# A 64 KB block of zeros written early to the rows that the first result overwrites, in a rotary-embedding kernel on Trainium2

## The chip, the cores and the metric

The kernel runs on one core of one Trainium2 chip. The metric is the device time of one execution in microseconds (us). "Span" is the profiled execution from its first to its last record; a run's time is about 1.8 us more than its span.

## The reference

```python
def reference(x, cos, sin):            # x: (8, 2048, 16, 64) f32; cos, sin: (2048, 32) f32
    x1, x2 = x[..., :32], x[..., 32:]
    cos, sin = cos[None, :, None, :], sin[None, :, None, :]
    return concatenate([x1 * cos - x2 * sin, x1 * sin + x2 * cos], axis=-1)
```

x has 67.1 MB, and so has the output. Each of the 8 batches is 8.39 MB in float32; the kernel keeps one batch in SBUF as float16, 4096 KB (128 partitions x 32 KB).

## The kernel before

The head of batch 0, sin and cos are loaded in float32 on the SyncE queue. Everything else is moved on the GpSimd queue, which converts float32 to float16 on the way in and back on the way out. ScalarE converts the head, sin and cos; VectorE does four passes per batch.

```python
    NBUF = 5
    ...
    head = const_pool.tile([P, JA, H, D], f32)
    x0 = x[0].rearrange("(p j) h d -> p j (h d)", j=J)
    nc.sync.dma_start(out=head..., in_=x0[:, 0:JA, :]...)              # 1 MB
    sin_f = const_pool.tile([P, J, Dh], f32)
    cos_f = const_pool.tile([P, J, Dh], f32)
    ...
    nc.sync.dma_start(out=sin_f, in_=sin.rearrange("(p j) d -> p j d", j=J))   # 256 KB
    nc.sync.dma_start(out=cos_f, in_=cos.rearrange("(p j) d -> p j d", j=J))   # 256 KB

    def load(b):  ...   # nc.gpsimd.dma_start: x[b] -> xt (f16), 4096 KB; batch 0 without its head
    def store(b, xt):
        nc.gpsimd.dma_start(out=out[b].rearrange("(p j) h d -> p (j h d)", j=J), in_=xt)
    def rotate(xt):     # four VectorE passes; the third is the cosine multiply
        ...
        nc.vector.tensor_mul(out=xw, in0=xw, in1=cos_b)
        nc.vector.tensor_add(out=xa, in0=xa, in1=v...)

    tiles = [load(b) for b in range(NBUF)]
    nc.scalar.copy(out=tiles[0][:, 0:JA, :, :]..., in_=head...)
    nc.scalar.copy(out=sin_h, in_=sin_f)
    nc.scalar.mul(out=neg_h, in_=sin_f, mul=-1.0)
    nc.scalar.copy(out=cos_h, in_=cos_f)
    for b in range(B):
        rotate(tiles[b])
        store(b, tiles[b])
        if b + NBUF < B:
            tiles.append(load(b + NBUF))
```

In the compiled order the GpSimd queue holds five loads, then store 0, store 1, load 5, load 6, store 2, store 3, load 7, stores 4 to 7. Load 5 waits for store 0 to land (its buffer comes free then), load 6 for store 1, load 7 for store 2.

## Time and profile before

| | before |
|---|---|
| median time (6 runs) | 318.21 us (317.96 to 318.41) |
| span of the profiled run | 316.1 us |
| VectorE busy | 209.2 us, 66% |
| DMA engines, both queues | 98.5% + 1.4% of 16 engines' span |
| read + written | 67.63 + 67.11 MB, 426 GB/s |

From the page of the kernel before: the span; busy time of the engines; the slices (one digit is the busy tenths of one fortieth of the span, here 7.9 us); then the DMA queues with packets, MB, and the share of 16 engines' span that their packets took.

```profile
span 316.1 us, 121 instructions
...
DVE 209.2 (66%) x32; ACT 4.9 (2%) x5; POOL 8.8 (3%) x20
...
DVE  0009799999999999999879999990009993000000
...
DMA  9899999999999999999999999999999999999996
...
q0 software_dynamic: 2304, 100.14, 98.5%
q1 hardware_dynamic: 432, 1.57, 1.4%
HBM read 67.63 MB, written 67.11 MB: 426 GB/s over the span
```

The DMA engines are full in all slices but the last, while VectorE (DVE) is idle in the first three and the last six, and in some between. The kernel is bound by the transfers. It follows that a wait on any other engine costs time only if the DMA queues run empty because of it.

DMA issues of the kernel before (output <- input, queue, count, KB each, median us from issue to landing):

```profile
head<-in_x_dram SPq DMA_DIRECT2D x1, 1024.0 KB, 4.8
sin_f<-in_sin_dram SPq DMA_DIRECT2D x1, 256.0 KB, 13.4
cos_f<-in_cos_dram SPq DMA_DIRECT2D x1, 256.0 KB, 31.8
out_dram<-xt POOLq DMA_DIRECT2D x8, 66.0
```

256 KB of cos need 31.8 us, over six times as long as 1 MB of head. The packet records in the trace tell why. There are eight data packets per engine in each of these transfers. (A record names the queue of a packet and not its engine. "Per engine" is here a sixteenth of all packets of a kind; the first or last 16 load or store packets by start are taken for one of each engine.) Head and most of sin pass before the engines take up the loads, between 5.2 and 5.7 us. After that, one packet of cos (2 KB, 96 ns) passes for each load packet (28 KB landed in SBUF, 2.13 us, later 32 KB and 2.43 us). The Trainium skill, "DMA: Bandwidth & Descriptors", section "Queues, rings and completion order", describes this: an engine goes round-robin between its queues, a packet at a time. Here the trace agrees.

Timeline of the kernel before (start, duration, engine, line, operation, and in brackets how long the engine was idle before and what ended it). L58 is a store, L51 a load, L70 the cosine multiply:

```profile
33.51 0.62 ACT L81 CAST cos_h<-cos_f 128x512 f16<-128x512 f32 x1 [17.74 <-DMA cos_f<-in_cos_dram]
34.16 8.69 DVE L70 TENSOR_TENSOR xt<-xt,cos_h 128x16384 f16<-128x16384 f16 x1 [1.75 <-ACT cos_h L81]
...
52.14 0.54 POOL L58 DMA_DIRECT2D out_dram<-xt  x1 [48.10 <-DVE xt L72]
...
78.12 0.54 POOL L58 DMA_DIRECT2D out_dram<-xt  x1 [25.44 <-DVE xt L72]
...
121.76 0.53 POOL L51 DMA_DIRECT2D xt<-in_x_dram  x1 [43.11 <-DMA out_dram<-xt]
...
263.88 0.53 POOL L58 DMA_DIRECT2D out_dram<-xt  x1 [50.50 <-DVE xt L72]
```

Store 0 is issued at 52.1 us, when VectorE is done with batch 0. But the packet records show the store's first packet only at 101.07 us: its descriptors stand in the same queue behind five loads. This distance of 49 us, less the time from an issue to its first packet, is the slack of store 0.

Who waited for whom (us in total, times, longest), first lines of the waits of the kernel before:

```profile
POOL out_dram L58 <- DVE xt L72: 136.3, 4, 50.5
POOL xt L51 <- DMA out_dram<-xt: 118.3, 3, 56.4
...
DVE xt L70 <- ACT cos_h L81: 1.7, 1, 1.7
```

### The profile page before, as it was taken

How to read it: one execution, taken by the hardware profiler on the slowest of the kernel's cores; microseconds unless marked ns; L12 is line 12 of the kernel's file. 1: busy time of each engine (PE TensorE's matmuls, PEld its weight loads, DVE VectorE, ACT ScalarE, POOL GpSimd, SP SyncE). 2: the span in 40 equal slices, each digit the busy share in tenths (PEclk: the TensorE clock that was granted, in tenths of full speed). 3: DMA queues.
4: the chain of work that ended last, by engine and by line, in shares of the span. 5: the costliest groups of instructions: out<-in, count | busy, mean ns of one | idle time of the engine just before them, and what ended most of it. 6: DMA issues, size and time to landing. Idle time of an engine off the chain costs nothing.

```text
span 316.1 us, 121 instructions
## 1 busy us (share of the span) xinstructions
DVE 209.2 (66%) x32; ACT 4.9 (2%) x5; POOL 8.8 (3%) x20
## 2 busy tenths in 40 slices
DVE  0009799999999999999879999990009993000000
ACT  4100000000000000000000000000000000000000
POOL 3000000000000000010000000100000000000000
DMA  9899999999999999999999999999999999999996
GB/s 277 182 261 208 199 236 228 199 199 265 199 199 265 398 506 423 398 336 261 199 199 224 373 398 398 506 423 265 203 328 398 398 448 481 398 398 506 423 398 265
DMA packets 2736, 101.71 MB, mean 322 GB/s; under 512 B 304, under 2 KB 304, under 8 KB 560
## 3 DMA queue, kind: packets, MB, share of 16 engines
q0 software_dynamic: 2304, 100.14, 98.5%
q1 hardware_dynamic: 432, 1.57, 1.4%
HBM read 67.63 MB, written 67.11 MB: 426 GB/s over the span
## 4 chain that ended last, share of the span: by engine, by line
issue 44%; DVE 14%; another core or an unknown queue 14%; DMA 10%; POOL 1%; SPq 0%; ACT 0%; POOLq 0%
DMA cos_f<-in_cos_dram 10%; DVE xt L70 6%; DVE xt L72 6%; DVE v L67 1%; DVE v L68 1%; POOL out_dram L58 1%; POOL xt L51 0%; ACT cos_h L81 0%; POOLq L112 0%; SPq L45 0%; SPq L36 0%; POOLq L58 0%
## 5 line engine op out<-in xcount | busy, mean ns | idle before, releaser
L70 DVE TENSOR_TENSOR xt<-xt,cos_h 128x16384 f16<-128x16384 f16 x8 | 69.5, 8692 | 2.0 <-ACT cos_h L81 1.7
L67 DVE TENSOR_TENSOR v<-xt,neg_h 128x8192 f16<-128x8192 f16 x8 | 35.4, 4426 | 52.2 <-DMA xt<-in_x_dram 52.0
L72 DVE TENSOR_TENSOR xt<-xt,v 128x16384 f16<-128x16384 f16 x8 | 69.5, 8692 | 0.3
L68 DVE TENSOR_TENSOR v<-xt,sin_h 128x8192 f16<-128x8192 f16 x8 | 35.4, 4419 | 0.0
L58 POOL DMA_DIRECT2D out_dram<-xt x8 | 4.3, 535 | 136.3 <-DVE xt L72 136.3
L51 POOL DMA_DIRECT2D xt<-in_x_dram x8 | 4.4, 559 | 119.1 <-DMA out_dram<-xt 118.3
L75 ACT CAST xt<-head 128x2048 f16<-128x2048 f32 x1 | 1.9, 1897 | 3.5 <-DMA head<-in_x_dram 3.5
L75 ACT ACT_TABLE_LOAD x1 | 1.3, 1283 | 0.7 <-PEq L101 0.7
L81 ACT CAST cos_h<-cos_f 128x512 f16<-128x512 f32 x1 | 0.6, 617 | 17.7 <-DMA cos_f<-in_cos_dram 17.7
L79 ACT CAST sin_h<-sin_f 128x512 f16<-128x512 f32 x1 | 0.6, 618 | 7.2 <-DMA sin_f<-in_sin_dram 7.2
L80 ACT ACTIVATE neg_h<-sin_f 128x512 f16<-128x512 f32 x1 | 0.6, 624 | 0.0
L101 POOL MEMSET const-float32-0.0<- 128x1 f32 x1 | 0.1, 98 | 0.2 <-issue 0.2
L101 POOL MEMSET const-bfloat16-1.0<- 128x1 bf16 x1 | 0.1, 101 | 0.0
L101 POOL MEMSET const-float32-1.0<- 128x1 f32 x1 | 0.1, 98 | 0.0
L101 POOL MEMSET const-uint8-127<- 128x1 uint8 x1 | 0.1, 98 | 0.0
## 6 DMA issues: line engine op xcount, KB each, us to landing
xt<-in_x_dram POOLq DMA_DIRECT2D x7, 4096.0 KB, 41.2
xt<-in_x_dram POOLq DMA_DIRECT2D x1, 3584.0 KB, 22.3
head<-in_x_dram SPq DMA_DIRECT2D x1, 1024.0 KB, 4.8
sin_f<-in_sin_dram SPq DMA_DIRECT2D x1, 256.0 KB, 13.4
cos_f<-in_cos_dram SPq DMA_DIRECT2D x1, 256.0 KB, 31.8
out_dram<-xt POOLq DMA_DIRECT2D x8, 66.0
```

The costliest lines, as they stand in the source:

```text
L51: nc.gpsimd.dma_start(out=xt[:, j0:J, :, :].rearrange("p j h d -> p (j h d)"), in_=x[b].rearrange("(p j) h d -> p j (h d)", j=J)[:, j0:J, ...
L58: nc.gpsimd.dma_start(out=out[b].rearrange("(p j) h d -> p (j h d)", j=J), in_=xt)
L67: nc.vector.tensor_mul(out=v[:, :, :, 0:Dh], in0=xt[:, :, :, Dh:D], in1=neg_b)
L68: nc.vector.tensor_mul(out=v[:, :, :, Dh:D], in0=xt[:, :, :, 0:Dh], in1=sin_b)
L70: nc.vector.tensor_mul(out=xw, in0=xw, in1=cos_b)
L72: nc.vector.tensor_add(out=xa, in0=xa, in1=v.rearrange("p j h d -> p (j h d)"))
L75: nc.scalar.copy(out=tiles[0][:, 0:JA, :, :].rearrange("p j h d -> p (j h d)"), in_=head.rearrange("p j h d -> p (j h d)"),)
L79: nc.scalar.copy(out=sin_h, in_=sin_f)
L80: nc.scalar.mul(out=neg_h, in_=sin_f, mul=-1.0)
L81: nc.scalar.copy(out=cos_h, in_=cos_f)
L101: nc = _bacc.Bacc("TRN2", target_bir_lowering=False, num_devices=1)
```

## The change

The result stays the same, as the zeros are overwritten. As far as the diff shows, the intent is to touch the output early, at a time when ScalarE's queue has nothing to do. What it costs, or gains, is asked here.

```diff
+    zero = const_pool.tile([P, 128], f32)
+    nc.vector.memset(zero, 0.0)
+    nc.scalar.dma_start(
+        out=out[0].rearrange("(p j) h d -> p (j h d)", j=J)[:, 0:128], in_=zero
+    )
     sin_f = const_pool.tile([P, J, Dh], f32)
```

Each of the 128 partitions writes 512 B. Store 0 writes the same bytes later, so the compiled store 0 gets one wait more, on the zeros' semaphore. The Trainium skill, "DMA: Bandwidth & Descriptors", section "Two DMAs through the same engine are not ordered", says that such a semaphore is the ordering that a kernel's author has; sharing a queue or an engine does not order the two writes. All other instructions keep their order on each engine. The line numbers after the change are higher by five (L70 becomes L75).

## The prediction

> **What bounds the kernel.** The 16 DMA engines. The page gives software queue q0 98.5% and hardware queue q1 1.4% of the engines' span; VectorE is busy 66% (209.2 us). 67.63 MB are read and 67.11 MB written: 426 GB/s over the 316.1 us span. The packet records add up to about 315.7 us per engine, so the span is the sum of the packets' times; the "issue" shares in the chain of waits are the GpSimd queue waiting for transfers in flight.
>
> **What the change does.** It adds a 128x128 memset on VectorE, idle until 23.65 us (timeline); a 64 KB transfer on the ScalarE queue, 128 rows of 512 B, eight per engine; and, in the compiled order, one wait: the first store also waits for the zeros to land. Nothing is removed; the order on every engine is otherwise the same.
>
> **Cost on the DMA engines.** In the packet records 8 KB packets of the head took 309 ns, 2 KB packets of sin/cos 84 ns. The line through these puts a 512 B packet at 28 ns (estimate): eight, with a completion packet of 9 to 22 ns, are 0.25 us per engine; perhaps 0.5 us if short writes are dearer. The engines are full from 2 us on, so this adds to the sum: +0.25 to +0.5 us.
>
> **The new wait.** The Trainium skill, "DMA: Bandwidth & Descriptors", section "Queues, rings and completion order", says an engine goes round-robin between its queues, a packet at a time. The trace agrees: after the loads start (first packet 5.2 us), one 2 KB packet passes per load packet of 2.13 us (later 2.43), so cos needs 31.8 us to land. The zeros should start at 2 to 2.5 us beside the head's packets and land by 5 to 7 us; caught behind load packets, by about 22 us. The first store becomes ready only at 51.6 us. So the wait is free. Even a late first store has room: its packets queue behind the first five loads, which fill the engines until 101 us (first store packet 101.1 us).
>
> **A side effect.** The zeros take engine time before the loads start. About 3 to 5 packets of sin/cos per engine then move behind load packets: sin lands at 21 to 25 us instead of 14.6, cos at 40 to 44 instead of 33.5, and the cosine multiply starts at 41 to 45 instead of 34.2. VectorE's early chain slides up to 10 us; the first two stores issue at about 60 and 87 instead of 52.1 and 78.1, both before 101 us. The third and fourth were issued only at 141.6 anyway, and the last (ready 263.6, its packets starting near 295) keeps slack. So this is absorbed: DMA never runs dry.
>
> **Predicted time: 318.5 us, range 318.0 to 319.3** (8 in 10). Faster by over 2%: 0.01; within 2%: 0.965; slower by over 2%: 0.025.
>
> **What would show each step.** A memset under 0.3 us near 1 us; zeros landing before 25 us; no wait of the first store put down to the zeros, but to the last add; cos landing later, the cosine multiply's idle time up from 1.75 us to around 10; DMA share still 98% or more; the sixth load still issued near 121.8 us; the last store landing 0.3 to 0.5 us later.
>
> **What would make it wrong.** Short strided writes costing far more than 28 ns; zeros landing after 52 us, or after 100 us, so that engines run dry before the first store; the slide of VectorE's chain exceeding its slack late; a fixed launch cost of a third DMA-issuing queue.

## The result, and the profile after

| | before | after |
|---|---|---|
| median time, 6 runs each | 318.21 us | 317.95 us |
| lowest to highest | 317.96 to 318.41 | 317.87 to 318.63 |
| ratio, 95% interval | | 0.9997, 0.9984 to 1.001 |
| span of the profiled run | 316.1 us | 316.1 us |

A ratio is the mean time of one kernel's fast runs over that of the other's fast runs of the same rounds, so it is not quite the ratio of the medians. The change is within noise: the interval reaches from 0.5 us less to 0.3 us more. The median is 0.05 us under the lower end of the predicted range.

The same lines of the page of the kernel after; q10 is the ScalarE queue:

```profile
span 316.1 us, 125 instructions
...
DVE 209.3 (66%) x33; ACT 4.9 (2%) x5; POOL 8.9 (3%) x20
...
DVE  0009179999999999999999999993009993000000
...
DMA  9899999999999999999999999999999999999996
...
q0 software_dynamic: 2304, 100.14, 98.4%
q1 hardware_dynamic: 432, 1.57, 1.4%
q10 hardware_dynamic: 144, 0.07, 0.1%
HBM read 67.63 MB, written 67.17 MB: 426 GB/s over the span
```

The DMA row has the same digits. In the DVE row the fifth digit fell from 7 to 1: that is the longer wait for cos. The memset adds 0.1 us to VectorE in this rounding, and the new queue took 0.1% of the engines' span.

DMA issues of the kernel after:

```profile
head<-in_x_dram SPq DMA_DIRECT2D x1, 1024.0 KB, 4.9
sin_f<-in_sin_dram SPq DMA_DIRECT2D x1, 256.0 KB, 19.9
cos_f<-in_cos_dram SPq DMA_DIRECT2D x1, 256.0 KB, 39.2
out_dram<-xt POOLq DMA_DIRECT2D x8, 59.6
out_dram<-zero ACTq DMA_DIRECT2D x1, 64.0 KB, 4.8
```

The zeros landed 4.8 us after their issue at 1.03 us, so at 5.8 us. Sin and cos landed 6.5 and 7.4 us later than before.

Timeline of the kernel after, the lines that answer to those of before and the two new ones:

```profile
0.84 0.17 DVE L41 MEMSET zero<- 128x128 f32 x1 [0.84 <-PEq L106]
1.03 0.40 ACTq L42 DMA_DIRECT2D out_dram<-zero  x1
...
40.86 0.62 ACT L86 CAST cos_h<-cos_f 128x512 f16<-128x512 f32 x1 [18.64 <-DMA cos_f<-in_cos_dram]
41.51 8.69 DVE L75 TENSOR_TENSOR xt<-xt,cos_h 128x16384 f16<-128x16384 f16 x1 [8.77 <-ACT cos_h L86]
...
59.49 0.54 POOL L63 DMA_DIRECT2D out_dram<-xt  x1 [55.44 <-DVE xt L77]
...
85.47 0.54 POOL L63 DMA_DIRECT2D out_dram<-xt  x1 [25.44 <-DVE xt L77]
...
121.76 0.54 POOL L56 DMA_DIRECT2D xt<-in_x_dram  x1 [35.76 <-DMA out_dram<-xt]
...
263.92 0.53 POOL L63 DMA_DIRECT2D out_dram<-xt  x1 [46.69 <-DVE xt L77]
```

Cos, the cosine multiply and stores 0 and 1 are all 7.35 us later. At load 5 nothing is left of that: it was issued at 121.76 us in both kernels, and store 7 at 263.92 us against 263.88.

Waits of the kernel after, first lines:

```profile
POOL out_dram L63 <- DVE xt L77: 143.6, 4, 55.4
POOL xt L56 <- DMA out_dram<-xt: 110.9, 3, 56.4
...
DVE xt L75 <- ACT cos_h L86: 8.8, 1, 8.8
```

No wait of a store was put down to the zeros. (ScalarE waited 1.5 us for the memset at the start.) The GpSimd queue waited 7.3 us longer for VectorE (143.6 against 136.3) and 7.4 us shorter for the stores' landing (110.9 against 118.3): a wait was exchanged for another.

**Where the packets' time went.** This table is from the packet records of the two traces. It has the mean start of the 16 engines' first load packets, of the last load packets of the first five loads, and of the first store packets, in us from the span's start.

| mean start of | before | after | difference |
|---|---|---|---|
| first load packets | 5.39 | 5.56 | +0.17 |
| last packets of the first five loads | 98.09 | 98.30 | +0.21 |
| first store packets | 101.47 | 101.52 | +0.05 |
| last store packets | 311.51 | 311.56 | +0.05 |

A 512 B packet took 27 ns, and eight of them with a completion packet of 9 ns are 0.225 us per engine. They are paid where they pass: the loads run 0.2 us late. Then, in this pair of traces, most of it is given back at one place, the turn from the last load packet to the first store packet. Between two neighbouring load packets, or store packets, the engines' mean starts lie 2.4 us apart. At this turn it was 3.38 us before and 3.22 us after, because the last load packet of each engine took about 3.4 us before (2.43 us is usual), and about 3.2 us after. From the first store packet on, both kernels need 210.04 us to the last one. (The experiments below show that this turn differs by 0.24 us between two traces of one kernel, so a difference of 0.16 us in it cannot be put down to the change.)

### The profile page after: what moved, and what is told of

Read it like the earlier page. It is cut to its first block, busy times and chain, and to the rows that moved or that the text cites. A ratio compares the mean times of both kernels' runs of the same rounds, so it can differ in the third digit from the quotient of the medians.

```text
span 316.1 us, 125 instructions
## 1 busy us (share of the span) xinstructions
DVE 209.3 (66%) x33; ACT 4.9 (2%) x5; POOL 8.9 (3%) x20
## 2 busy tenths in 40 slices
DMA packets 2880, 101.78 MB, mean 322 GB/s; under 512 B 320, under 2 KB 448, under 8 KB 704
## 3 DMA queue, kind: packets, MB, share of 16 engines
q0 software_dynamic: 2304, 100.14, 98.4%
## 4 chain that ended last, share of the span: by engine, by line
issue 44%; DVE 14%; DMA 12%; another core or an unknown queue 11%; POOL 1%; SPq 0%; ACT 0%; POOLq 0%
DMA cos_f<-in_cos_dram 12%; DVE xt L75 6%; DVE xt L77 6%; DVE v L72 1%; DVE v L73 1%; POOL out_dram L63 1%; POOL xt L56 1%; ACT cos_h L86 0%; POOLq L117 0%; SPq L50 0%; SPq L36 0%; POOLq L63 0%
## 5 line engine op out<-in xcount | busy, mean ns | idle before, releaser
L75 DVE TENSOR_TENSOR xt<-xt,cos_h 128x16384 f16<-128x16384 f16 x8 | 69.5, 8692 | 9.0 <-ACT cos_h L86 8.8
L63 POOL DMA_DIRECT2D out_dram<-xt x8 | 4.3, 536 | 143.6 <-DVE xt L77 143.6
L56 POOL DMA_DIRECT2D xt<-in_x_dram x8 | 4.4, 561 | 111.7 <-DMA out_dram<-xt 110.9
## 6 DMA issues: line engine op xcount, KB each, us to landing
xt<-in_x_dram POOLq DMA_DIRECT2D x7, 4096.0 KB, 41.5
cos_f<-in_cos_dram SPq DMA_DIRECT2D x1, 256.0 KB, 39.2
```

The lines of the kernel that those rows point to most:

```text
L56: nc.gpsimd.dma_start(out=xt[:, j0:J, :, :].rearrange("p j h d -> p (j h d)"), in_=x[b].rearrange("(p j) h d -> p j (h d)", j=J)[:, j0:J, ...
```

## The experiments

Most kernels are the changed kernel with one thing altered. In swq_last both queue and target differ, dry4 has both early and late zeros, and read64k reads instead of writing. Those with zeros to the last batch or with a larger block of them still give the right result, since a store overwrites them; all twelve were correct. The times of the kernel before differ between the three calls, which ran on different chips (medians 317.9, 318.2 and 318.65 us), so a kernel is compared with others of its own call only.

My theory: the packets' time adds to the span, and the wait is free as long as the zeros land before the first five loads have drained. Rivals: short packets are free; any wait of the first store on the zeros costs; or a late store is always given back.

### 1. Ten times the packets, wait on the last store: z10_last

```diff
-        out=out[0].rearrange("(p j) h d -> p (j h d)", j=J)[:, 0:128], in_=zero
+        out=out[B - 1].rearrange("(p j) h d -> p j (h d)", j=J)[:, 0:10, 0:128],
+        in_=zero.unsqueeze(1).to_broadcast([P, 10, 128]),
```

> Ten times the zeros (128 rows x 10 pieces of 512 B, 640 KB, one transfer on the ScalarE queue), aimed at the rows of the last batch, so that only the last store, ready near 264 us, has to wait for them. Theory (the span is the sum of the packets' times, a 512 B packet adds its 27 ns on each engine): 80 packets x 27 ns = 2.2 us more, about 320.3 us, ratio 1.006 to 1.008; one packet of 512 B passes per load or store packet, so they land near 190 to 210 us. Rival (the time of short packets is hidden, because something other than the engines' packet time is the limit, which would also give the change's +0.0): ratio within 0.002 of 1. If ten pieces travel as one packet, eight packets of 5 KB: about 1.6 us and landing near 20 us.

Measured: 319.56 us (319.53 to 319.65, 5 runs) beside 317.9 us, ratio 1.0048, 1.0035 to 1.0062. The 80 packets did add time, 1.7 us, but less than the 2.2 us that I expected. Their records were 38 ns each (40 ns beside load packets), 3.06 us per engine. Not all of that is in the span: the turn at the first store was no longer than any other step (2.48 us), so 0.9 us of the old turn was gone, and the packet records overlap. The zeros landed 158 us after their issue, earlier than expected, because some 13 of the 80 packets per engine had passed by 5.6 us.

### 2. The same packets, wait on the first store: z10_first

```diff
-        out=out[0].rearrange("(p j) h d -> p (j h d)", j=J)[:, 0:128], in_=zero
+        out=out[0].rearrange("(p j) h d -> p j (h d)", j=J)[:, 0:10, 0:128],
+        in_=zero.unsqueeze(1).to_broadcast([P, 10, 128]),
```

> The same ten-fold zeros, aimed at the first batch, so that the first store waits for them. If each piece is a packet of its own they are caught behind the loads and land only when the loads have drained, near 101 to 103 us. Theory: the 2.2 us of the packets as in the twin aimed at the last batch, and on top a dry stretch of the engines between the end of the loads and the first store's first packet, 2 to 5 us; in all 322.5 to 325.5 us, the first store's wait put down to the zeros, 40 us and more. Rival (late first store is given back later, since later waits have slack): same as the twin.

Measured: 321.53 us (321.48 to 321.57, 4 runs), ratio 1.011, 1.0096 to 1.0124; 1.97 us more than the twin. The total is 1 us under my range, and the wait's part just under the 2 to 5 us that I gave the dry stretch. The longest wait, from the waits of z10_first:

```profile
POOL out_dram L64 <- DMA out_dram<-zero: 100.1, 1, 100.1
```

The issue of the first two stores, from its timeline:

```profile
104.16 1.07 POOL L64 DMA_DIRECT2D out_dram<-xt  x2 [100.11 <-DMA out_dram<-zero]
```

The first store was issued at 104.16 us, 41.2 us later than in the twin (62.96 us), and the kernel lost 2 us.

### 3. and 4. The wait alone, and its control: swq_first and swq_last

The 64 KB are issued on the GpSimd queue behind the five loads. By my theory sin and cos are then not pushed back by them.

```diff
-    nc.scalar.dma_start(
-        out=out[0].rearrange("(p j) h d -> p (j h d)", j=J)[:, 0:128], in_=zero
-    )
     ...
     tiles = [load(b) for b in range(NBUF)]
+    nc.gpsimd.dma_start(
+        out=out[0].rearrange("(p j) h d -> p (j h d)", j=J)[:, 0:128], in_=zero
+    )                       # swq_last: out[B - 1]
```

> The original 64 KB of zeros to the first batch, but issued on the GpSimd queue after the five first loads. Theory: no slide of sin/cos (cos lands at 33.5 us as before the change), zeros land near 101 us behind the loads, the first store is issued then instead of 52 us, and the engines run dry until its first packet: 2 to 5 us, in all 320.4 to 323.5 us. Rival (a late first store is absorbed as the slide of VectorE was): 318.0 to 318.7 us.

> Control of the previous one: same zeros, same GpSimd queue, but to the rows of the last batch, so that the first store does not wait. Both theories: 318.0 to 318.7 us, first store issued at about 52 us. If it is slower than that, it is the extra GpSimd transfer and not the wait that costs.

Measured: swq_first 319.53 us (319.35 to 319.7, 5 runs), ratio 1.0047, 1.0035 to 1.006. swq_last 317.85 us (317.78 to 318.0, 5 runs), ratio 0.9995, 0.9983 to 1.0008. The wait therefore costs 1.68 us when the zeros land behind the loads, a little less than my range had it, and the extra transfer alone costs nothing that can be seen. Cos was converted at 33.41 us in swq_last, as before, but at 35.85 in swq_first, where I had expected 33.5. The short packets there are behind the loads, so this is scatter: the same kernel run again as dry0 (below) converted cos at 33.16. The first two stores in the timeline of swq_first:

```profile
102.35 1.06 POOL L60 DMA_DIRECT2D out_dram<-xt  x2 [97.76 <-DMA out_dram<-zero]
```

The first store in the timeline of swq_last:

```profile
52.04 0.54 POOL L60 DMA_DIRECT2D out_dram<-xt  x1 [47.45 <-DVE xt L74]
```

In swq_first the slices show the hole, in the 13th digit of the DMA row of the page:

```profile
DMA  9899999999996999999999999999999999999996
```

The packet records give its size. The slowest engine's last load packet ended at 101.26 us and the zeros' packet at 101.42. The store was issued at 102.35, its first packet started at 103.46, and the mean start of the 16 first store packets was 103.52 against 101.61 in swq_last. From the end of the zeros' last packet to the first packet of the store are 2.04 us, 0.93 of it before the store's issue and 1.11 after. The Trainium skill, "DMA: Bandwidth & Descriptors", section "Anatomy of one DMA — SWDGE (gpsimd) path", gives a fixed cost of about 2.0 us per transfer; the total agrees here.

So the first store was issued 50.3 us later, and the kernel lost 1.7 us. A first store issued at 62 us, in z4_last below, costs nothing that can be seen; issued at 102 us, it costs 1.7. No run lies closely between, so that the cost begins near 101 us is argued from the end of the loads and not shown.

### 5. Four times the packets: z4_last

```diff
-        out=out[0].rearrange("(p j) h d -> p (j h d)", j=J)[:, 0:128], in_=zero
+        out=out[B - 1].rearrange("(p j) h d -> p j (h d)", j=J)[:, 0:4, 0:128],
+        in_=zero.unsqueeze(1).to_broadcast([P, 4, 128]),
```

> Four times the zeros (32 packets of 512 B per engine), aimed at the last batch. They should land near 65 to 75 us, before the engines turn from loads to stores (98 us). In the ten-fold run the 512 B packets took 38 ns each, 3.1 us per engine, but the last load packet of each engine, 0.94 us longer than its like in the kernel before, was no longer than the others, and the net was 1.7 us. Theory (packet time adds up, and the long last load packet goes only if short packets still pass at the turn): 32 x 38 ns = 1.2 us minus at most 0.3, 318.8 to 319.2 us, long last load packets still there (0.6 us or more). Rival (cost simply in proportion to the ten-fold run, nothing to do with the turn): 0.66 us, 318.4 to 318.7 us.

Measured: 318.21 us (318.09 to 318.39, 5 runs) beside 318.2, ratio 0.9998, 0.9986 to 1.0011. Both expectations were too high. The packet records show 32 x 29 ns = 0.93 us per engine. The last load packets started at 98.97 us, 0.88 later than in the trace of before, and the first store packets at 102.02, 0.55 later. The turn had shrunk to 3.05 us, although the zeros had landed at 50.9 us (I had expected 65 to 75), long before it. Note that the trace of before is from another call; what the runs of this call show is that nothing of 0.35 us or more (the interval's upper end) was left in the time.

### 6. and 11. A wait that ends late but in time: sp_after_cos, run twice

```diff
-    nc.scalar.dma_start(... in_=zero)
     ...
     nc.sync.dma_start(out=cos_f, in_=cos.rearrange("(p j) d -> p j d", j=J))
+    nc.sync.dma_start(
+        out=out[0].rearrange("(p j) h d -> p (j h d)", j=J)[:, 0:128], in_=zero
+    )
```

> The same zeros to the first batch, issued on the SyncE queue behind cos. Theory: sin and cos land as before the change (about 13.4 and 32 us from their issue), the cosine multiply idles about 1.75 us again, the zeros land at 52 to 57 us, so the first store waits for them for 0 to 5 us; time within 0.4 us of before, as its packets queue behind the loads until 101 us. Rival (any wait of the first store on the zeros costs): slower by that wait.

Measured: 318.96 us (317.88 to 319.06, 4 runs) beside 318.2, ratio 1.0022, 1.0007 to 1.0038. The run with the trace took 317.88 us, the other three 318.89 to 319.06. The cosine multiply idled 3.8 us, not 1.75. The first store in the timeline of sp_after_cos:

```profile
55.71 0.54 POOL L63 DMA_DIRECT2D out_dram<-xt  x1 [51.67 <-DMA out_dram<-zero]
```

It really was the zeros that the first store waited for, 1.6 us longer than for VectorE's last pass as it lies in this trace (after that alone, store 0 would have been issued at about 54.1 us), and this run was not slower than before. But three runs were.

> The kernel of sp_after_cos again. There one run of four took 317.88 us and was the one with a trace; the other three took 318.89 to 319.06. If that is a property of the kernel, most of these runs lie near 319.0 and a trace of one shows where: theory, in the last load packet of each engine at the turn to stores, 1.6 us or more too long instead of 0.82; rival, the first store's wait on the zeros, ending later than 55.7 us, or an idle stretch of the engines. If it was a passing state of that chip, all lie at 317.7 to 318.5.

Measured: 318.78 us (318.25 to 318.88, 5 runs) beside 318.65 us of the kernel before (318.08 to 318.88), ratio 1.0004, 0.999 to 1.0018. Here the kernel before itself spread up to 318.88. The trace fell on the fastest run again (318.25 us). In it, too, the first store waited for the zeros, until 53.23 us, and the last load packets were 0.6 us too long, not 1.6 us or more. So the 0.7 us of the first time did not come back relative to before, and no trace shows what it was. It stays open; these runs do not support a cost of that wait, and the first call alone would have.

### 7. Reading instead of writing: read64k

```diff
-    zero = const_pool.tile([P, 128], f32)
-    nc.vector.memset(zero, 0.0)
+    dummy = const_pool.tile([P, 128], f32)
     nc.scalar.dma_start(
-        out=out[0].rearrange("(p j) h d -> p (j h d)", j=J)[:, 0:128], in_=zero
+        out=dummy, in_=x[0].rearrange("(p j) h d -> p (j h d)", j=J)[:, 0:128]
     )
```

> Instead of writing zeros, the ScalarE queue reads the same 128 x 512 B from x into an unused tile: the same packets, no memset, no write, no new wait. Theory: the same slide (cos lands 38 to 44 us, the cosine multiply idles 7 to 11 us), time within 0.4 us of before. The long last load packets (0.94 us per engine too long in before, 0.79 with the zeros): if it is an early write that shortens them, about 0.94 here; if it is the slide, about 0.79.

Measured: 317.99 us (317.94 to 318.22, 5 runs) beside 318.2, ratio 0.9992, 0.998 to 1.0005. The slide is there with neither memset nor write nor wait. From the DMA issues of read64k:

```profile
cos_f<-in_cos_dram SPq DMA_DIRECT2D x1, 256.0 KB, 36.7
...
dummy<-in_x_dram ACTq DMA_DIRECT2D x1, 64.0 KB, 5.0
```

The first cosine multiply in its timeline:

```profile
39.00 8.69 DVE L74 TENSOR_TENSOR xt<-xt,cos_h 128x16384 f16<-128x16384 f16 x1 [6.06 <-ACT cos_h L85]
```

So the slide comes from short packets passing before the loads start; that they carry zeros to the output does not matter. This is more than scatter: in the six traces without early short packets the multiply starts at 33.7 to 36.5 us, in the three with eight per engine at 39.0 to 41.5 (head_last, where cos comes first, aside). It is a little smaller here, though: the multiply idled 6.1 us, against the 7 to 11 that I had expected. The last load packets were 0.55 us per engine too long, less than both figures in the expectation. An early write is thus not needed to shorten the turn. The run does not tell what does.

### 8. The head behind sin and cos: head_last

```diff
-    nc.sync.dma_start(out=head..., in_=x0[:, 0:JA, :]...)
     zero = ...; memset; nc.scalar.dma_start(... in_=zero)
     nc.sync.dma_start(out=sin_f, ...)
     nc.sync.dma_start(out=cos_f, ...)
+    nc.sync.dma_start(out=head..., in_=x0[:, 0:JA, :]...)
```

> The change, with the head's load moved behind sin and cos on the SyncE queue. In the changed kernel the zeros' first packet came only at 4.7 us, when the head's packets were through, 3.7 us after the issue, and not in turn with them. Theory A (an engine finishes the descriptors it has already taken from one queue before it turns to another): the zeros start at 2.2 to 3.3 us here. Theory B (the ScalarE queue needs 3.7 us to start): 4.5 us or later. Sin and cos land by 5 us, the cosine multiply idles under 0.1 us, head lands at 7 to 13 us. If VectorE's early chain mattered the time would fall; theory: within 0.4 us of before.

Measured: 318.08 us (317.89 to 318.1, 4 runs) beside 318.2, ratio 0.9992, 0.9979 to 1.0006. DMA issues of head_last:

```profile
head<-in_x_dram SPq DMA_DIRECT2D x1, 1024.0 KB, 24.4
sin_f<-in_sin_dram SPq DMA_DIRECT2D x1, 256.0 KB, 2.6
cos_f<-in_cos_dram SPq DMA_DIRECT2D x1, 256.0 KB, 3.0
...
out_dram<-zero ACTq DMA_DIRECT2D x1, 64.0 KB, 2.5
```

Zeros, sin and cos all landed by 4.2 us, and the cosine multiply did not wait. The zeros' first packet came at 2.59 us, as theory A said, when the first engine was through with sin (its completion packet came at 2.58): the queue does not need 3.7 us to start. In read64k, where ScalarE issued in the same moment as SyncE, the first short packet came at 2.37 us, among the packets of the head. In the changed kernel the zeros were issued 0.29 us after the head and came only behind its eight packets. That fits an engine which finishes what it has already taken from a queue, but no record shows the taking itself. (read64k also reads where the zeros write, and no run separates that from the moment of issue.)

I was wrong on the head: it landed at 26.0 us, not by 13. Here the loads' first packets came at 3.4 us instead of 5.2, and the head's first packet only at 5.6, so that every packet of it had a load packet beside it. It also shows that in the other kernels the loads were held up at the start by the head's packets and not by their own issue. Batch 0 then waited for the head instead of cos. The time stayed, which shows once more that the early chain of VectorE does not set it.

### 9. and 10. Short packets on quieter ground: dry0 and dry4

dry0 is swq_first under a new name. dry4 adds the early zeros of z4_last.

```diff
+    nc.scalar.dma_start(                                   # dry4 only
+        out=out[B - 1].rearrange("(p j) h d -> p j (h d)", j=J)[:, 0:4, 0:128],
+        in_=zero.unsqueeze(1).to_broadcast([P, 4, 128]),
+    )
     ...
     tiles = [load(b) for b in range(NBUF)]
+    nc.gpsimd.dma_start(                                   # both
+        out=out[0].rearrange("(p j) h d -> p (j h d)", j=J)[:, 0:128], in_=zero
+    )
```

> The same kernel as swq_first, as the ground line for dry4 on the same chip: 319.2 to 319.8 us, a spread under 0.4 us. Its loads have drained before the first store's packets come, so the long last load packets[...] are absent, which leaves a quieter ground to weigh short packets on.

> dry0, with four times the change's zeros on the ScalarE queue as well, early, to the last batch: 32 packets of 512 B and a completion packet per engine, 0.95 us by the records of z4_last. Theory (packet times add to the span, and in the changed kernel and in z4_last a shorter turn from loads to stores gave most of it back): 0.7 to 1.1 us above dry0. Rival (short packets are free): within 0.25 us of dry0.

Measured: dry0 320.06 us (319.85 to 320.2), dry4 320.24 us (320.16 to 320.25), 5 runs each, beside 318.65 us of the kernel before. dry0 lies 0.26 us above the window that I gave it. dry4 took 0.18 us more than dry0, where I expected 0.7 to 1.1. The rival's number is the right one. From the packet records of the two profiled runs (spans 318.1 and 318.5 us; that of dry0 is the fastest of its five, so this pair differs by 0.39 us and not by 0.18):

| us | dry0 | dry4 | difference |
|---|---|---|---|
| records of the early zeros per engine | 0 | 0.93 | +0.93 |
| first load packets, mean start | 5.38 | 5.78 | +0.40 |
| last packets of the first five loads, mean start | 98.15 | 98.99 | +0.84 |
| the last of these to end, on the slowest engine | 101.39 | 101.78 | +0.39 |
| first store packets, mean start | 103.66 | 104.05 | +0.39 |

The average engine was 0.84 us later, the slowest only 0.39 us, and the store follows the slowest, because it waits for a transfer that all 16 engines carry. In dry0 the engines were spread over 1.05 us when they ended their loads (100.34 to 101.39), in dry4 over 0.53 (101.25 to 101.78). In this one pair of traces, then, part of the short packets went into the waiting of the faster engines.

### 12. The change without its wait: zero_last

```diff
-        out=out[0].rearrange("(p j) h d -> p (j h d)", j=J)[:, 0:128], in_=zero
+        out=out[B - 1].rearrange("(p j) h d -> p (j h d)", j=J)[:, 0:128], in_=zero
```

> The change with one part undone: the same 64 KB of zeros at the same moment, aimed at the last batch, so the first store no longer waits for them and the last store does. Theory: nothing moves: cos lands at about 41 us, the first store is issued at 59 to 61 us (set by VectorE, not by the zeros), time 317.8 to 318.5 us. If the wait cost anything in the change, the first store is issued earlier than there.

Measured: 318.16 us (317.96 to 318.54, 5 runs) beside 318.65, ratio 0.9987, 0.9974 to 0.9999. The first store in the timeline of zero_last:

```profile
57.04 0.54 POOL L63 DMA_DIRECT2D out_dram<-xt  x1 [53.00 <-DVE xt L77]
```

It waited for VectorE here too. It was issued 2.45 us earlier than in the changed kernel, so my expected window was missed; cos had landed that much earlier (36.8 us from issue against 39.2), and in this trace, too, the store follows VectorE at once: from the start of the first cosine multiply to the issue of store 0 are 17.97 us here, 17.98 in the changed kernel and 17.98 before. So the added wait held up nothing in the change. No experiment gave a version that clearly beats both kernels.

## Why the prediction was right or wrong

- **The bound: right.** DMA stayed full (98.4% + 1.4% + 0.1%), and every change of VectorE's early chain (cos multiply at 34.2, 41.5, 39.0, 44.4 us in before, after, read64k and z4_last) left the time alone. One reason that I gave is weaker than it looks: that the packet records add up to the span (315.7 against 316.1 us) is partly chance. In the trace of before packets pass only from 1.74 to 314.28 us, which is 312.5 us, so the records overlap by about 1% (load packets of 2.43 us start 2.41 us apart).
- **The wait is free: right.** The zeros landed at 5.8 us (predicted 5 to 7), 53 us before the first store became ready at 58.9 us. That waiting costs once the zeros land behind the loads is shown; that the edge lies near 101 us is not, as no run lies between a store at 63 us and one at 102. Landing behind the loads cost 1.68 us in swq_first against swq_last, and 1.97 us in z10_first against z10_last.
- **The slide: right in kind; its size, near the low end, is in part luck.** Sin landed at 21.1 us (predicted 21 to 25), cos at 40.8 (40 to 44), the multiply started at 41.5 (41 to 45) after 8.8 us of idling (around 10), and stores 0 and 1 were issued at 59.5 and 85.5 (60 and 87). Load 5 was issued at 121.76 us in both. But in zero_last, with the same packets at the same moment, cos was converted at 38.4 us and the multiply started at 39.1, below these ranges. The reason for the slide was only half right: I had 3 to 5 packets per engine fall behind load packets. On average it was 0.7 (5.8 of sin's eight packets had started by 5.7 us before, 5.1 after). But a landing follows the slowest engine: the engines completed sin between 9.5 and 14.3 us before, and between 5.7 and 20.8 us after. In zero_last 6.5 of the eight had started by 5.7 us, more than before, and sin still landed later (19.0 us): the mean does not carry the slide.
- **The zeros' start: wrong, without effect.** I had them at 2 to 2.5 us "beside the head's packets". The first came at 4.7 us, behind them. They landed in the predicted window all the same.
- **"The engines are full from 2 us on, so this adds to the sum: +0.25 to +0.5 us": this term was mis-sized.** The packets are as short as estimated (27 ns against 28) and cost 0.17 to 0.21 us up to the last load packet. But only 0.05 us was left after the turn to the stores, and the medians differ by -0.26 us, with an interval that allows -0.5 to +0.3. The step that was mis-sized is the addition of an average engine's packet times. The change alone cannot show it, as its interval also holds the +0.25 us; the larger doses do: 0.95 us of records per engine left less than 0.35 us in z4_last, 0.93 us left 0.18 in dry4, and 3.06 us left 1.7 us in z10_last. So short packets are not free either. The mean lateness of the loads did not pass through the turn whole: 0.88 us became 0.55 in the trace of z4_last (against the trace of before), and 0.84 became 0.39 in dry4. In dry4 the slowest engine's lateness explains it. In the changed kernel, where the queue never runs dry, the last load packet itself was shorter by 0.16 us in this pair of traces, and whether the change does that, and why, is open. The two traces of one and the same kernel, sp_after_cos, have turns of 3.25 and 3.01 us, so 0.05 us means nothing.
- **The total: 318.5 us predicted, 317.95 us measured.** The forecast of no visible change held. The range was drawn upward of before for a cost that cannot be seen here, and the median fell just under it. Runs of one kernel differ by 0.45 to 0.76 us, so these six could not have told +0.25 us from none.

## What to carry to other kernels

When transfers bound a kernel, price an added wait by asking when the DMA queue behind it would run dry, not by how long the engine waits: here a store held back by 50 us cost 1.7 us. A few short packets before a stream of large ones can push small transfers back by a large packet each, which matters only if someone on the critical path waits for them. Do not add packet times to the microsecond: the slowest engine and the turn from loads to stores decide what is left of them.

## What the Trainium skill lacked or had wrong

- "DMA: Bandwidth & Descriptors", section "Queues, rings and completion order", has the round-robin between queues (confirmed: one 2 KB packet per load packet of 2.13 to 2.43 us). The section does not say what happens to a transfer that comes a little after another: the zeros, issued 0.29 us after the head, came behind all eight head packets per engine (4.7 us), while the read issued in the same moment took turns with them (from 2.37 us).
- The same section gives packets of about 9 to 17 descriptors as typical. In the records here each row of a ScalarE or SyncE transfer was a packet of its own (512 B, 2 KB, 8 KB), eight per engine and transfer, and the engines changed queue after single rows of cos. The GpSimd queue did put the eight rows of 512 B of an engine into one packet of 4096 B (172 ns, against 8 x 27 = 216 ns).
- No page has the turn from loads to stores: the last load packet of each engine took about 2.8 to 3.8 us instead of 2.43 in the runs where stores stood in the queue behind it, and in z10_last, where short packets still passed there, it did not. Its length changed from run to run by some tenths of a us, which is as much as a small change costs.
- Neither lacking nor wrong: the fixed cost of about 2 us per GpSimd transfer, in "DMA: Bandwidth & Descriptors", section "Anatomy of one DMA — SWDGE (gpsimd) path", was met, with 2.04 us from the end of the zeros' last packet to the first packet of the store that waited for it.
